# A Strassen-type transformer kernel: another order of the seven products, split token sums, block-diagonal gates, other store queues

## The chip, the cores and the metric

The kernel runs on one core of a Trainium2 chip. The metric is the device time of one execution in microseconds (us); the median of three runs counts. The engines are TensorE (PE, matrix products; PEld is its weight load), VectorE (DVE), ScalarE (ACT), GpSimd (POOL) and SyncE (SP), which issues most transfers; ACT and POOL issue some too. PSUM is the memory that TensorE writes, in 8 banks of 128 partitions x 512 fp32.

## The reference

There are two blocks of a network over one sequence of 1024 tokens of width 1024.

```python
h = rms_norm(x, norm1_g);  z = h @ w_in            # 1024 -> 3584
lru_x, lru_gate, sc_b, sc_c, sc_x = split(z)
lru_x = causal_dwconv(lru_x, lru_conv_w) + lru_conv_b
r = sigmoid(lru_x . wa + ba);  i = sigmoid(lru_x . wx + bx)   # 16 heads, 64 x 64 blocks
h_t = a_t * h_{t-1} + sqrt(1 - a_t^2) * (i * lru_x)_t         # a from r and lambda
y_lru = h * gelu(lru_gate);  y_sc = sc_b * causal_dwconv(sc_c * sc_x, sc_conv_w)
x = x + concat(y_lru, y_sc) @ w_out
u = causal_dwconv(rms_norm(x, norm2_g) @ w_up, ffn_conv_w);  gate, up = split(u)   # 1024 -> 6144
x = rms_norm(x + (gelu(gate) * up) @ w_down, final_g)
# second block: h = x @ w_in_2 gives q and kv of low rank, a pooled branch and two gates;
# attention of 4 heads with rope; layer_norm(alpha * x + concat(y_a, y_b) @ w_out_2)
```

## The kernel before

**Precision.** Each fp32 operand is held as a rounded part (hi, a CAST on ACT) and a rest (lo, a subtraction on DVE), and a product is three matmuls: hi·hi, hi·lo, lo·hi. `products` (L107) issues them at L110.

**Pairs.** The three stages of wide projections (the mix of block one, 14 pairs `wl*`, `ws*`, `wb*`; the ffn's `w_up`, 24 pairs `wf0` to `wf23`; block two's `w_in`, 9 pairs) work on pairs of 128 output columns by Strassen's scheme in Winograd's form: seven products of half width, each 12 matmuls of 128x512 into one PSUM bank. Products 1 and 2 share a bank (x), 6, 7 and 4 another (y), 5 and 3 a third (z). Later products of a bank add to what stands there, so what stands there must be read out (`evac`) before the next product of the bank starts. The tokens' operands (`Hop`) stay for the whole stage: product 1 reads B11, 2 reads B21 (both of tokens 0 to 511 alone), 5 reads T1, 6 T2, 7 T3, 4 T4 and 3 B22, sums in which tokens 512 to 1023 take part. The weights' operands are made for each pair: `load` fetches quarters, and their sums are formed in the DMA, by adding transfers that POOL issues (`sum`, L257 and L258, and L273). Product 5's operand is the tile `s`; once its lo part is done, an adding transfer turns `s` into 6's operand, and after 6's lo part another one turns it into 3's.

**Order of work.** Everything is emitted step by step, and each engine runs its own instructions in that order. `Pairs.step` emits the loads and sums of later pairs, the read-out of the product before, the hi and lo parts of the operand that is AHEAD products later, the product, and `tick()`, which emits the tasks that `later(n, ...)` put n steps ahead: convolutions, gates, scans, stores. ORDER is the order of the products in a pair, `prep_seq` that of the operands; the first two pairs of a stage run interleaved.

**Transitions.** `transition` leads into each stage: per tile of 128 tokens `norm.a` and `norm.b` (norm) and `norm.T` (transpose on PE, then the operands' parts). `T` of tiles 0 to 3 makes B11 and B21, `T` of tiles 4 to 7 the five others, nine DVE operations each (L443 to L462).

**Gates and late stages.** An lru pair's two gates multiply 64-row heads; the operands are stacked, hi over lo, so that eight matmuls do (`gates`), and eight sigmoids of 64 partitions read them (L666, L667). After the second stage `pooled_rows` fetches four tiles `yb` and four `wob`, splits each (`split`, L103 and L104) and multiplies them; `low_norm` (L1090) scales the fetched `lq`.

## Time and profile before

| | |
|---|---|
| median of 3 runs | 1858.32 us (1853.94 to 1858.72) |
| profiled execution | 1859.06 us, its span 1857.3 us |
| mean granted TensorE clock | 0.950 |
| PE / PEld / DVE / ACT / POOL busy | 1653.0 / 1351.0 / 1212.0 / 855.0 / 360.2 us |

Start and end of the span leave 1.8 us of the profiled time outside. Busy shares are means over stages with different limits, so they say little alone; the stages by time are: transition one to 77 us, the mix to about 404, its output rows to 524, transition two to 577, the ffn's pairs to 1060, its output rows to 1340, transition three to 1360, block two's pairs to 1538, the pooled rows to 1610, then q, k, v, attention and the last product. A share of granted clock of 1.00 is 2.4 GHz, 0.50 is 1.2 GHz.

### The profile page before, as it was taken

How to read it: one execution, taken by the hardware profiler on the slowest of the kernel's cores; microseconds unless marked ns; L12 is line 12 of the kernel's file. 1: busy time of each engine (PE TensorE's matmuls, PEld its weight loads, DVE VectorE, ACT ScalarE, POOL GpSimd, SP SyncE). 2: the span in 40 equal slices, each digit the busy share in tenths (PEclk: the TensorE clock that was granted, in tenths of full speed). 3: DMA queues.
4: the chain of work that ended last, by engine and by line, in shares of the span. 5: the costliest groups of instructions: out<-in, count | busy, mean ns of one | idle time of the engine just before them, and what ended most of it. 6: DMA issues, size and time to landing. Idle time of an engine off the chain costs nothing.

```text
span 1857.3 us, 20276 instructions
## 1 busy us (share of the span) xinstructions
PE 1653.0 (89%) x7315; PEld 1351.0 (73%) x7315; DVE 1212.0 (65%) x1729; ACT 855.0 (46%) x1290; POOL 360.2 (19%) x373
## 2 busy tenths in 40 slices
...
GB/s 208 87 101 85 114 128 107 72 182 226 125 108 89 164 125 135 143 148 144 125 134 144 166 334 123 102 54 10 124 127 129 184 72 283 215 108 266 92 99 118
DMA packets 272830, 255.36 MB, mean 137 GB/s; under 512 B 18422, under 2 KB 238420, under 8 KB 272724
## 3 DMA queue, kind: packets, MB, share of 16 engines
...
q14 instruction: 47, 0.39, 0.1%
...
## 4 chain that ended last, share of the span: by engine, by line
PE 45%; issue 22%; DMA 11%; DVE 11%; ACT 7%; POOL 3%; SPq 1%; POOLq 0%; DVEq 0%; ACTq 0%
PE o L110 22%; PE wu L110 4%; PE wob L110 2%; PE wl L110 2%; PE wq L110 2%; PE wga L110 2%; PE s L110 2%; PE ws L110 1%; PE qn L110 1%; PE wb L110 1%; PE wkv L110 1%; DVE B L443 1%; DVE T L443 1%; PE qr L110 1%; DVE ffc L758 1%
## 5 line engine op out<-in xcount | busy, mean ns | idle before, releaser
L110 PE MATMUL o<-yw 128*128 128x512 f32 x1632 | 375.3, 390 | 0.0
L110 PEld LDWEIGHTS o<-yw 128*128 128x128 f32 x1632 | 305.6, 188 | 63.6 <-DVE yw L524 0.8
L564 DVE TENSOR_TENSOR x<-x,o 128x512 f32<-128x512 f32 x160 | 108.6, 684 | 132.5 <-PE o L110 132.3
L523 ACT CAST yw<-yraw 128x1024 fp32r<-128x1024 f32 x34 | 35.7, 1051 | 174.4 <-PE o L110 152.4
L407 ACT ACTIVATE xn<-x 128x1024 f32<-128x1024 f32 x24 | 25.5, 1064 | 61.1 <-DVE x L564 54.3
L761 ACT ACTIVATE ffc<-ffc 128x1024 f32<-128x1024 f32 x24 | 25.4, 1059 | 58.5 <-DVE ffc L758 58.5
L524 DVE TENSOR_TENSOR yw<-yraw,yw 128x1024 fp32r<-128x1024 f32 x34 | 43.3, 1274 | 12.8 <-ACT yw L523 12.7
L524 DVE TENSOR_TENSOR yw<-wraw,yw 128x1024 fp32r<-128x1024 f32 x34 | 41.4, 1218 | 1.3 <-ACT yw L523 1.3
L436 PE MATMUL T<-cst,xn 128*128 128x128 f32 x128 | 20.7, 319 | 24.0 <-DVE xn L423 24.0
L523 ACT CAST yw<-wraw 128x1024 fp32r<-128x1024 f32 x34 | 35.8, 1053 | 11.2 <-DMA wraw<-in_w_out_dram 8.6
L110 PE MATMUL wob<-wobl,ybh 128*128 128x512 f32 x64 | 26.3, 410 | 15.3 <-DVE wobl L104 15.3
L1460 POOL TENSOR_TENSOR rt<-rt,lng 128x1024 f32<-128x1024 f32 x6 | 14.4, 2398 | 125.3 <-ACT rt L1459 125.3
L436 PEld LDWEIGHTS T<-cst,xn 128*128 128x128 f32 x128 | 18.0, 167 | 26.8 <-DVE xn L423 18.6
L668 POOL TENSOR_TENSOR i<-i,xc 128x1024 f32<-128x1024 f32 x8 | 19.6, 2448 | 77.7 <-ACT i L667 73.5
L110 PE MATMUL wob<-wobh,ybh 128*128 128x512 f32 x64 | 26.0, 413 | 9.3 <-ACT wobh L103 9.3
L257 POOL DMA_DIRECT2D wu3s<-in_w_in_dram x1 | 1.3, 1282 | 167.7 <-DMA wu3s<-in_w_in_dram 167.7
L110 PE MATMUL o<-PT,Vh 128*128 128x256 f32 x160 | 30.2, 287 | 4.0 <-DVE PT L1367 3.3
L1346 ACT ACTIVATE sc<-sc,st 128x256 f32<-128x256 f32 (+3 forms) x32 | 26.3, 823 | 15.2 <-DVE st L1345 15.1
L442 ACT CAST B<-T 128x512 fp32r<-128x512 f32 x36 | 20.8, 590 | 26.3 <-PE T L436 14.3
L417 POOL TENSOR_SCALAR ss<-ss 128x1 f32<-128x1 f32 x24 | 8.1, 339 | 117.7 <-ACT ss L408 116.9
L764 DVE TENSOR_TENSOR ffc<-ffc,ffc 128x1024 f32<-128x1024 f32 x24 | 29.3, 1222 | 1.9 <-ACT ffc L761 1.9
L110 PEld LDWEIGHTS o<-PT,Vh 128*128 128x128 f32 x160 | 25.3, 191 | 5.8 <-DVE PT L1367 4.2
...
## 6 DMA issues: line engine op xcount, KB each, us to landing
...
```

Source lines behind the costliest of these rows:

```text
L110: PE.matmul(ps, lhsT=l, rhs=r, start=(first and j == 0), stop=(last and j == n - 1), skip_group_check=not first)
L407: A.activation(xn, X[t], AF.Square, accum_out=ss[:, 0:1])
L436: PE.transpose(ps[:, k * P:(k + 1) * P], src[:, c * P:(c + 1) * P], ident)
L442: A.copy(Hop[m][:, 0, :, sl], src)
L443: V.tensor_tensor(Hop[m][:, 1, :, sl], src, f(Hop[m][:, 0, :, sl]), SUB)
L523: A.copy(s[:, j], src)
L524: V.tensor_tensor(s[:, j + 1], src, f(s[:, j]), SUB)
L564: V.tensor_tensor(X[t][:, ns], X[t][:, ns], ps, ADD)
L668: G.tensor_tensor(i, i, st.pop("xc"), MUL)
L761: A.activation(st["g"], st["g"], AF.Gelu_apprx_tanh)
L764: V.tensor_tensor(st["u"], st["u"], st["g"], MUL)
L1346: A.activation(s, s, AF.Exp, scale=QK_SCALE, bias=st[:, 1:2], accum_out=st[:, 2:3])
```

## The change

- Within a pair the products run 1, 6, 2, 7, 5, 4, 3 and no longer 6, 1, 5, 7, 2, 3, 4; operands are made 5 products ahead and not 6, in the order 5, 1, 2, 6, 7, 4, 3; loads and sums are emitted at other steps. Bank x is read out on ACT alone and the others on DVE alone, so product 6's read-out moves from ACT to DVE, product 1's loses its DVE addition, and the copy of product 5 and its later subtraction (L311, L317) fall away for all pairs but the first two of a stage. Between two products of one bank there now stands one other product, before there were two.
- In the first two pairs of a stage product 2 has a bank of its own (`apart`), and the order is 1, 2, 5, 3, 6, 7, 4, the two pairs in turn.
- `T` of tiles 4 to 7 makes only the parts of products 5 and 3; the new `T2` makes those of 6, 7 and 4, after two more steps of the products.
- The gates' weights are block-diagonal 128x128 tiles, with zeros put in by POOL; the gates take 12 matmuls, 4 sigmoids of 128 partitions and one split of `xc`, and their tasks come two steps earlier. The second and third pair of the mix change places.
- Stores of block two's pairs go out over POOL's or ACT's queue, not SP's.
- `pooled_rows` splits into four tiles of the pool H, not into 16 of the pool U.

```diff
-    ORDER = (6, 1, 5, 7, 2, 3, 4)
+    ORDER = (1, 6, 2, 7, 5, 4, 3)
...
-            if m in FIRST:
+            new = m in FIRST or m == 2 and self.apart
+            if new:
                 self.ps[g] = PB(self.nm)
+            self.bank[m] = self.ps[g]
             w, h = self.op.pop(m), Hop[m]
             terms = []
             for k in range(4):
                 terms += [(w[:, 0, k], h[:, 0, k]), (w[:, 0, k], h[:, 1, k]), (w[:, 1, k], h[:, 0, k])]
-            products(self.ps[g], terms, m in FIRST, True)
+            products(self.ps[g], terms, new, True)
...
             if m == 1:
                 A.copy(zb[:, n0], ps)
-                if 6 in self.seen:
-                    V.tensor_tensor(za[:, n1], za[:, n1], ps, ADD)
+            elif m == 2 and self.apart:
+                V.tensor_tensor(za[:, n0], ps, zb[:, n0], ADD)
             elif m == 2:
                 A.copy(za[:, n0], ps)
             elif m == 6:
-                if 1 in self.seen:
-                    V.tensor_tensor(za[:, n1], zb[:, n0], ps, SUB)
-                else:
-                    A.activation(za[:, n1], ps, AF.Copy, scale=-1.0)
+                V.tensor_tensor(za[:, n1], (za[:, n1] if 3 in self.seen else zb[:, n0]), ps, SUB)
...
+            elif 6 in self.seen:
+                V.tensor_tensor(za[:, n1], za[:, n1], ps, ADD)
             else:
-                V.tensor_tensor(za[:, n1], za[:, n1], ps, ADD)
+                V.tensor_tensor(za[:, n1], ps, zb[:, n0], ADD)
...
-        AHEAD = 6
+        AHEAD = 5
...
+            for p in pairs[:2]:
+                p.apart = True
+            self.seq = [(p, m) for m in (1, 2, 5, 3, 6, 7, 4) for p in pairs[:2]]
             self.seq += [(p, m) for p in pairs[2:] for m in ORDER]
-            early = (5, 1, 7, 2, 6, 4, 3)
-            self.prep_seq = [(p, m) for m in (1, 5, 2, 7, 6, 4, 3) for p in pairs[:2]]
-            self.prep_seq += [(p, m) for p in pairs[2:] for m in early]
+            self.prep_seq = [(p, m) for m in (1, 5, 2, 6, 3, 7, 4) for p in pairs[:2]]
+            self.prep_seq += [(p, m) for p in pairs[2:] for m in (5, 1, 2, 6, 7, 4, 3)]
...
-            self.load((g + 12) // 7 + 1)
-            self.sums((g + 9) // 7 + 1)
+            self.load(g // 7 + 3)
+            if g >= 3:
+                self.sums((g - 3) // 7 + 3)
...
-                Hop[6] = HB("T2")
-                Hop[5], Hop[7], Hop[4], Hop[3] = HT2("T1"), HT2("T3"), HT2("T4"), HT2("B22")
-            r = self.raw.pop(j)
+                Hop[5], Hop[3] = HT2("T1"), HT2("B22")
+            r = self.raw[j]
             q = U("hsum", F32, (P, 2, 4, P))
             V.tensor_tensor(q[:, 0], r[:, 0], v[0], SUB)
+            parts(5, q[:, 0])
+            parts(3, v[1])
             V.tensor_tensor(q[:, 1], v[1], q[:, 0], ADD)
-            parts(3, v[1])
-            for h in range(2):
-                V.tensor_tensor(r[:, h], r[:, h], q[:, 1], SUB)
-            parts(5, q[:, 0])
+            self.st[t] = q, parts
+
+        def T2(self, t):
+            q, parts = self.st.pop(t)
+            if t == 4:
+                Hop[6], Hop[7], Hop[4] = HB("T2"), HT2("T3"), HT2("T4")
+            r = self.raw.pop(t % 4)
             parts(6, q[:, 1])
+            V.tensor_tensor(r[:, 0], r[:, 0], q[:, 1], SUB)
             parts(7, r[:, 0])
+            V.tensor_tensor(r[:, 1], r[:, 1], q[:, 1], SUB)
             parts(4, r[:, 1])
...
         norm.T(7)
+        pairs.step()
+        pairs.step()
+        for t in range(4, NT):
+            norm.T2(t)
...
+            t = gwt[j] = U("gates", F32, (P, 8, P))
+            G.memset(t, 0.0)
             w = I[nm][0].rearrange("(c two) i j -> two i c j", two=2)
-            for rows_, half, col in zip((LOW, HIGH), (0, 1), cols):
-                SY.dma_start(t[rows_, :, col], w[half])
-
-    def stacked(src, rows_, hi, lo=None):
-
-        other = HIGH if rows_ == LOW else LOW
-        lo_t = hi if lo is None else lo
-        A.copy(hi[rows_], src[rows_])
-        V.tensor_tensor(lo_t[other], src[rows_], f(hi[rows_]), SUB)
-        if lo is not None:
-            A.copy(hi[other], src[rows_])
-            V.tensor_tensor(lo[rows_], src[rows_], f(hi[rows_]), SUB)
+            for half, r in enumerate((LOW, HIGH)):
+                SY.dma_start(t[r, :, r], w[half])
...
+            gw = U("gw", F32R, (P, 2, 2, P))
+            for j in range(2):
+                A.copy(gw[:, 0, j], gwt[j][:, c])
+                V.tensor_tensor(gw[:, 1, j], gwt[j][:, c], f(gw[:, 0, j]), SUB)
...
+        def cut():
+            st["xs"] = split(st["xc"], "xs")
 
         def gates():
             st["ps"] = [[PB("ga"), PB("ga")] for _ in range(2)]
+            (xh, xl), gw = st.pop("xs"), st.pop("gw")
             for j in range(2):
-                x = st.pop(f"xs{j}")
                 for n in range(2):
                     ns = slice(n * 512, (n + 1) * 512)
-                    products(st["ps"][j][n], [(st["gw"][:, 2 * j + part, :], x[:, ns]) for part in range(2)])
+                    products(st["ps"][j][n], [(gw[:, 0, j], xh[:, ns]), (gw[:, 0, j], xl[:, ns]), (gw[:, 1, j], xh[:, ns])])
...
+            for j, dst in enumerate((r, i)):
                 for n in range(2):
                     ns = slice(n * 512, (n + 1) * 512)
-                    ps = st["ps"][j][n]
-                    A.activation(r[own, ns], ps[own], AF.Sigmoid, bias=vcol(40 + c)[own])
-                    A.activation(i[own, ns], ps[other], AF.Sigmoid, bias=vcol(48 + c)[other])
+                    A.activation(dst[:, ns], st["ps"][j][n], AF.Sigmoid, bias=vcol(40 + 8 * j + c))
...
+            later(2, lambda: tap(zx, 1))
+            later(3, lambda: (tap(zx, 2), gelu(zg)))
             later(4, lambda: tap(zx, 3))
-            later(5, lambda: cut(0))
-            later(6, lambda: cut(1))
-            later(9, gates)
-            later(10, lru_1)
-            later(12, lru_2)
-            later(13, lru_3)
-            later(15, lru_4)
+            later(5, cut)
+            later(7, gates)
+            later(8, lru_1)
+            later(10, lru_2)
+            later(11, lru_3)
+            later(12, lru_4)
+            later(13, lru_5)
...
-    order = "L0 L1 S0 L2 S1 L3 B0 L4 S2 L5 L6 S3 L7 B2"
+    order = "L0 S0 L1 S1 L2 L3 B0 L4 S2 L5 L6 S3 L7 B2"
...
-            store(YB_d[g], t)
+            store(YB_d[g], t, G)
...
-            store(GA_d[h + j], z)
+            A.dma_start(GA_d[h + j], z)
...
-            y[e] = split(y[e], "yb")
-            w[e] = split(w[e], "wob")
+            s = HT("yw", F32R, (P, 4, 1024))
+            for j, src in ((0, y[e]), (2, w[e])):
+                A.copy(s[:, j], src)
+                V.tensor_tensor(s[:, j + 1], src, f(s[:, j]), SUB)
+            y[e], w[e] = (s[:, 0], s[:, 1]), (s[:, 2], s[:, 3])
```

On ACT, where pair 16's products of the ffn run (`COPY` reads out a bank; L266 before and L260 after are the hi parts; `wf17s` is the tile that the transfers add to). Before, with product 1's read-out of pair 16 at the top:

```order
L293 COPY wf16z_6291<-wf_856_6296 128x512
L266 CAST wf17op_6324<-wf17a_6171 128x512
L761 ACTIVATE ffc_6310<-ffc_6310 128x1024
L311 COPY wf16m_863_6340<-wf_862_6326 128x512
L266 CAST wf17op_6343<-wf17s_6173 128x512
L266 CAST wf17op_6361<-wf17a_6171 128x512
L266 CAST wf17op_6380<-wf17s_6173 128x512
L266 CAST wf17op_6398<-wf17b_6176 128x512
L297 COPY wf16z_6290<-wf_856_6296 128x512
L266 CAST wf17op_6415<-wf17s_6173 128x512
L754 ACTIVATE ffc_6430<-wf16z_6291,fvec 128x1024
```

and of the change, with product 1's read-out of pair 16 at the top:

```order
L289 COPY wf16z_6175<-wf_832_6159 128x512
L260 CAST wf16op_6178<-wf16s_5872 128x512
L750 ACTIVATE ffc_6194<-wf15z_6035,fvec 128x1024
L260 CAST wf17op_6199<-wf17s_6011 128x512
L260 CAST wf17op_6219<-wf17a_6009 128x512
L260 CAST wf17op_6236<-wf17a_6009 128x512
L293 COPY wf16z_6174<-wf_832_6159 128x512
L757 ACTIVATE ffc_6194<-ffc_6194 128x1024
L260 CAST wf17op_6254<-wf17s_6011 128x512
L260 CAST wf17op_6272<-wf17s_6011 128x512
L260 CAST wf17op_6296<-wf17b_6014 128x512
L750 ACTIVATE ffc_6311<-wf16z_6175,fvec 128x1024
```

The hi parts of pair 17 stand in the order of `prep_seq`: before 5, 1, 7, 2, 6, 4, 3, in the change 5, 1, 2, 6, 7, 4. Before, that of product 3 (the last from `wf17s`) stands three rows behind that of product 6; now it stands past the end of these rows, behind pair 17's own read-out of product 1, and that of product 6 stands behind pair 16's read-out of product 2.

On PE, at transition two (`T<-cst,xn` are transposes of the last tiles, `wf` is the bank; B_515 and B_506 are B11, B_516 and B_507 are B21, T_545 and T_563 are T2, T_546 and T_536 are T1). Before:

```order
L110 MATMUL wf_556_3902<-B_515_3663,wf0op_3527 128x512 x12
L436 MATMUL T_3915<-cst,xn_3778 128x128 x4
L436 MATMUL T_3920<-cst,xn_3778 128x128 x4
L110 MATMUL wf_563_3946<-B_515_3663,wf1op_3530 128x512 x12
L436 MATMUL T_3959<-cst,xn_3823 128x128 x4
L436 MATMUL T_3964<-cst,xn_3823 128x128 x4
L110 MATMUL wf_556_3902<-B_516_3664,wf0op_3545 128x512 x12
L110 MATMUL wf_563_3946<-B_516_3664,wf1op_3897 128x512 x12
L110 MATMUL wf_575_4031<-T_545_3845,wf0op_3995 128x512 x12
L110 MATMUL wf_577_4050<-T_545_3845,wf1op_4012 128x512 x12
L110 MATMUL wf_579_4067<-T_546_3846,wf0op_3535 128x512 x12
L110 MATMUL wf_582_4085<-T_546_3846,wf1op_3541 128x512 x12
```

and of the change:

```order
L110 MATMUL wf_546_3807<-B_506_3583,wf0op_3447 128x512 x12
L431 MATMUL T_3820<-cst,xn_3698 128x128 x4
L431 MATMUL T_3825<-cst,xn_3698 128x128 x4
L110 MATMUL wf_553_3843<-B_506_3583,wf1op_3450 128x512 x12
L431 MATMUL T_3856<-cst,xn_3743 128x128 x4
L431 MATMUL T_3861<-cst,xn_3743 128x128 x4
L110 MATMUL wf_560_3880<-B_507_3584,wf0op_3465 128x512 x12
L110 MATMUL wf_562_3900<-B_507_3584,wf1op_3805 128x512 x12
L110 MATMUL wf_567_3928<-T_536_3765,wf0op_3455 128x512
L110 MATMUL wf_570_3954<-T_536_3765,wf1op_3461 128x512
L110 MATMUL wf_567_3928<-T_536_3765,wf0op_3455 128x512 x11
L110 MATMUL wf_570_3954<-T_536_3765,wf1op_3461 128x512 x11
```

Product 2 writes other banks (`wf_560`, `wf_562`) than product 1 (`wf_546`, `wf_553`), and the products that follow it are those of T1, before they were those of T2.

On DVE, at the pooled rows (L104 and L1134 are lo parts, L1090 and L1086 the scaling of `lq`). Before:

```order
L313 TENSOR_TENSOR wga2z_10582<-wga_1414_10564,wga2z_10582 128x512
L1090 SCALAR_TENSOR_TENSOR lq_10750<-lq_10750,vec,linv_10748 128x1024
L1090 SCALAR_TENSOR_TENSOR lq_10752<-lq_10752,vec,linv_10748 128x1024
L1090 SCALAR_TENSOR_TENSOR lq_10754<-lq_10754,vec,linv_10748 128x1024
L1090 SCALAR_TENSOR_TENSOR lq_10756<-lq_10756,vec,linv_10748 128x1024
L104 TENSOR_TENSOR ybl_10767<-yb_10732,ybh_10766 128x1024
L104 TENSOR_TENSOR wobl_10771<-wob_10734,wobh_10770 128x1024
L104 TENSOR_TENSOR ybl_10799<-yb_10736,ybh_10798 128x1024
L104 TENSOR_TENSOR wobl_10803<-wob_10738,wobh_10802 128x1024
```

and of the change:

```order
L307 TENSOR_TENSOR wga2z_10418<-wga2z_10418,wga_1388_10472 128x512
L1134 TENSOR_TENSOR yw_10603<-yb_10569,yw_10603 128x1024
L1134 TENSOR_TENSOR yw_10603<-wob_10571,yw_10603 128x1024
L1134 TENSOR_TENSOR yw_10632<-yb_10573,yw_10632 128x1024
L1134 TENSOR_TENSOR yw_10632<-wob_10575,yw_10632 128x1024
L1134 TENSOR_TENSOR yw_10661<-yb_10577,yw_10661 128x1024
L1134 TENSOR_TENSOR yw_10661<-wob_10579,yw_10661 128x1024
L1134 TENSOR_TENSOR yw_10690<-yb_10581,yw_10690 128x1024
L1134 TENSOR_TENSOR yw_10690<-wob_10583,yw_10690 128x1024
L1086 SCALAR_TENSOR_TENSOR lq_10587<-lq_10587,vec,linv_10585 128x1024
L1086 SCALAR_TENSOR_TENSOR lq_10589<-lq_10589,vec,linv_10585 128x1024
```

The four scalings of `lq` stood ahead of the first lo part; now they stand behind the eighth.

## Rows read from the trace of the kernel before

**Rows 1.** Busy time of each engine by stretch. Columns: stretch in us, its length, busy us (instructions) of PE, PEld, DVE, ACT and POOL, granted clock, share of the DMA engines' time, GB/s.
```profile
0.00:77.44 77.44, 39.31 (x163) 32.55 (x164) 45.24 (x77) 40.69 (x79) 23.70 (x54) 0.69 0.67 154
77.44:404.00 326.56, 281.20 (x1151) 223.43 (x1150) 230.65 (x276) 219.94 (x314) 93.63 (x60) 0.94 0.53 101
...
524.00:577.06 53.06, 41.53 (x195) 34.08 (x194) 49.01 (x80) 34.97 (x68) 11.86 (x44) 0.87 0.37 115
577.06:1060.00 482.94, 452.93 (x1956) 367.60 (x1955) 326.37 (x438) 216.14 (x329) 112.79 (x87) 0.99 0.69 137
...
1360.00:1540.00 180.00, 178.17 (x786) 147.20 (x784) 111.77 (x152) 83.34 (x129) 34.70 (x27) 1.00 0.65 135
1540.00:1610.00 70.00, 47.18 (x192) 38.15 (x192) 31.62 (x27) 14.66 (x14) 0.00 (x0) 0.80 0.70 259
```

**Rows 2.** Waits of PE in the ffn's stretch (577 to 1060), by what ended them: us in total, times, longest. The first of twenty rows of this kind, one for each of pairs 3 to 23 but one.
```profile
PE wf L110 <- DVE wf8z L295: 2.9, 1, 2.9
```

**Rows 3.** PE in order of time around pair 17 of the ffn: start, us, engine, line, operation, output and inputs, count, and in brackets the idle time before and what ended it.
```profile
918.44 2.88 PE L110 MATMUL wf<-T,wf17op 128*128 128x512 f32 x12
...
921.16 2.88 PE L110 MATMUL wf<-B,wf17op 128*128 128x512 f32 x12
...
930.97 5.78 PE L110 MATMUL wf<-B,wf17op 128*128 128x512 f32 x24 [1.48 <-DVE wf17z L295]
```

**Rows 4.** DVE, POOL and ACT in the same stretch, columns as above, put in order of time.
```profile
913.63 0.68 DVE L271 TENSOR_TENSOR wf17op<-wf17s,wf17op 128x512 fp32r<-128x512 f32 x1
...
914.61 1.28 POOL L273 DMA_DIRECT2D wf17s<-in_w_up_dram  x1 [3.40 <-DVE wf17op L271]
...
920.83 0.62 ACT L266 CAST wf17op<-wf17s 128x512 fp32r<-128x512 f32 x1 [7.04 <-DMA wf17s<-in_w_up_dram]
...
921.48 0.69 DVE L271 TENSOR_TENSOR wf17op<-wf17s,wf17op 128x512 fp32r<-128x512 f32 x1 [5.96 <-ACT wf17op L266]
...
930.23 0.68 DVE L295 TENSOR_TENSOR wf17z<-wf17z,wf 128x512 f32<-128x512 f32 x1
```

**Rows 5.** Transfers: from issue to landing of the adding transfers of L273 at 900 to 935 us (three of them), and the median for pair 21's four issues.
```profile
DMA to landing us min/median/max: 4.3/4.6/6.2
...
wf21s<-in_w_up_dram POOLq DMA_DIRECT2D x4, 256.0 KB, 6.5
```

**Rows 6.** The transitions: waits of PE in transition one (columns as in rows 2), PE in order of time in transition two (columns as in rows 3), and the waits in transition three.
```profile
PE wl L110 <- ACT wl0z L293: 6.7, 1, 6.7
PE wl L110 <- ACT wl1z L293: 6.3, 1, 6.3
...
551.19 2.98 PE L110 MATMUL wf<-B,wf1op 128*128 128x512 f32 x12
...
561.30 5.43 PE L110 MATMUL wf<-B,wf0op 128*128 128x512 f32 x12 [6.25 <-ACT wf0z L293]
...
572.00 5.21 PE L110 MATMUL wf<-B,wf1op 128*128 128x512 f32 x12 [5.28 <-ACT wf1z L293]
...
593.40 2.88 PE L110 MATMUL wf<-B,wf0op 128*128 128x512 f32 x12
...
PE wu L110 <- ACT wu3z L293: 6.4, 1, 6.4
PE wkv L110 <- ACT wkvz L293: 5.8, 1, 5.8
```

**Rows 7.** A stretch of transition two by engine (columns as in rows 1), and ACT's read-out of product 1 of pair 0 (columns as in rows 3). The stretch begins with DVE's first sum for tile 4 (L458).
```profile
549.66:575.73 26.07, 14.54 (x53) 11.17 (x53) 26.05 (x44) 15.77 (x30) 3.65 (x8) 0.76 0.38 85
...
560.67 0.58 ACT L293 COPY wf0z<-wf 128x512 f32<-128x512 f32 x1
```

**Rows 8.** Waits of PE in the mix (77 to 404 us), columns as in rows 2: the longest, and the longest of two other kinds.
```profile
PE ws L110 <- ACT ws1op L266: 9.4, 1, 9.4
PE ws L110 <- DVE ws2z L295: 4.2, 1, 4.2
...
PE ws L110 <- ACT ws2z L302: 3.1, 1, 3.1
```

**Rows 9.** ACT in the mix: groups of equal shape, with busy us, mean ns, and idle time before them with what ended it; the last row is the cast L103 at the pooled rows, with min, median and max ns.
```profile
L667 ACT ACTIVATE i<-ga,vec 64x512 f32<-64x512 f32 x28 | 19.1, 684 | 1.7 <-DVE sco L718 1.3
...
L615 ACT CAST xs<-xc 64x1024 fp32r<-64x1024 f32 x14 | 14.6, 1046 | 17.6 <-DVE xc L641 13.2 <-PE ws L110 4.3
...
L103 ACT CAST ybh<-yb x4: 1044/1044/1044, 1545.1 to 1553.2; 128x1024 fp32r<-128x1024 f32 x4
```

**Rows 10.** ACT, PE and DVE at the pooled rows, columns as in rows 3.
```profile
1545.13 1.04 ACT L103 CAST ybh<-yb 128x1024 fp32r<-128x1024 f32 x1 [5.14 <-DMA yb<-YB]
...
1554.51 1.04 ACT L103 CAST wobh<-wob 128x1024 fp32r<-128x1024 f32 x1 [0.29 <-DMA wob<-in_w_out_dram]
...
1547.51 1.65 PE L110 MATMUL wob<-wobh,ybh 128*128 128x512 f32 x3 [9.34 <-ACT wobh L103]
...
1557.08 3.78 DVE L1090 SCALAR_TENSOR_TENSOR lq<-lq,vec,linv 128x1024 f32<-128x1024 f32 x3 [18.18 <-DMA lq<-LQ]
...
1564.46 0.80 PE L110 MATMUL wob<-wobl,ybh 128*128 128x512 f32 x1 [15.30 <-DVE wobl L104]
...
1570.12 0.39 PE L110 MATMUL wob<-wobl,ybh 128*128 128x512 f32 x1
...
1609.81 0.39 PE L110 MATMUL wob<-wobh,ybl 128*128 128x512 f32 x1
```

More of the change, by code (lines that the diff above doesn't have):

```diff
@@ L238, in __init__ @@
             self.ap, self.cols, self.nm, self.done = ap, (c0, c1), nm, done
-            self.op, self.ps, self.z, self.seen = {}, {}, None, []
+            self.op, self.ps, self.z, self.seen, self.apart, self.bank = {}, {}, None, [], False, {}
         def load(self):
@@ L282, in product @@
                 terms += [(w[:, 0, k], h[:, 0, k]), (w[:, 0, k], h[:, 1, k]), (w[:, 1, k], h[:, 0, k])]
-            products(self.ps[g], terms, m in FIRST, True)
+            products(self.ps[g], terms, new, True)
         def evac(self, m):
-            ps = self.ps[GROUP[m]]
+            ps = self.bank.pop(m)
             n0, n1 = slice(0, 512), slice(512, 1024)
@@ L322 @@
     class Pairs:
-        AHEAD = 6
+        AHEAD = 5
         def __init__(self, pairs):
             self.pairs = pairs
-            self.seq = [(p, m) for m in (1, 2) for p in pairs[:2]]
-            self.seq += [(p, m) for m in (6, 5, 7, 3, 4) for p in pairs[:2]]
+            for p in pairs[:2]:
+                p.apart = True
+            self.seq = [(p, m) for m in (1, 2, 5, 3, 6, 7, 4) for p in pairs[:2]]
             self.seq += [(p, m) for p in pairs[2:] for m in ORDER]
-            early = (5, 1, 7, 2, 6, 4, 3)
-            self.prep_seq = [(p, m) for m in (1, 5, 2, 7, 6, 4, 3) for p in pairs[:2]]
-            self.prep_seq += [(p, m) for p in pairs[2:] for m in early]
+            self.prep_seq = [(p, m) for m in (1, 5, 2, 6, 3, 7, 4) for p in pairs[:2]]
+            self.prep_seq += [(p, m) for p in pairs[2:] for m in (5, 1, 2, 6, 7, 4, 3)]
             self.n_load, self.n_sum, self.n_prep, self.n_prod, self.n_evac = 0, 0, 0, 0, 0
@@ L485, in transition @@
         norm.T(7)
+        pairs.step()
+        pairs.step()
+        for t in range(4, NT):
+            norm.T2(t)
+            pairs.step()
     class Rows:
@@ L604, in gate_weights_load, with store @@
     def gate_weights_load():
-        t = gwt["raw"] = U("gates", F32, (P, 8, P))
-        for nm, cols in (("lru_wa", (LOW, HIGH)), ("lru_wx", (HIGH, LOW))):
+        for j, nm in enumerate(("lru_wa", "lru_wx")):
+            t = gwt[j] = U("gates", F32, (P, 8, P))
+            G.memset(t, 0.0)
             w = I[nm][0].rearrange("(c two) i j -> two i c j", two=2)
-            for rows_, half, col in zip((LOW, HIGH), (0, 1), cols):
-                SY.dma_start(t[rows_, :, col], w[half])
-    def stacked(src, rows_, hi, lo=None):
-        other = HIGH if rows_ == LOW else LOW
-        lo_t = hi if lo is None else lo
-        A.copy(hi[rows_], src[rows_])
-        V.tensor_tensor(lo_t[other], src[rows_], f(hi[rows_]), SUB)
-        if lo is not None:
-            A.copy(hi[other], src[rows_])
-            V.tensor_tensor(lo[rows_], src[rows_], f(hi[rows_]), SUB)
+            for half, r in enumerate((LOW, HIGH)):
+                SY.dma_start(t[r, :, r], w[half])
     stored = set()
-    def store(dst, t):
+    def store(dst, t, E=SY):
         def go():
-            SY.dma_start(dst, t)
+            E.dma_start(dst, t)
             stored.add(id(dst))
```

32 lines of the change are left out of this document (8 added, 24 removed).

## Prediction

> **What bounds the kernel now.** I read the busy times by stretch first. They tell the reader to look at five places and to leave the rest. In the second block's pairs PE works 178.2 of 180 us at full clock [rows 1]: nothing is to be gained there, only lost. In the ffn's pairs it stands idle 482.9 - 452.9 = 30.0 us, in the mix 326.6 - 281.2 = 45.4 us, at the pooled rows 70.0 - 47.2 = 22.8 us with a granted clock of 0.80, and in transition two 53.1 - 41.5 = 11.5 us at 0.87 [rows 1]. So PE bounds the kernel, and what a change is worth is the idle time, and the low clock behind it, that it takes from PE.
>
> Then the waits. In the ffn nearly every pair has one wait of the same kind: PE stands before product 2 until DVE has added product 1 from the bank (L295) [rows 2]; in pair 17 it is 1.48 us [rows 3]. DVE in order of time shows why it is late. The lo part of product 6 is done at 914.3, POOL issues the adding transfer at 914.61, and ACT's next hi part from that tile waits until 920.83, 7.04 us; DVE then waits 5.96 us for it, and all that stands behind it is late, L295 too, at 930.23 [rows 4]. The landing is what ends last: 4.3 to 6.2 us from issue, with 6.5 as a later pair's median [rows 5].
>
> In transition two PE waits for ACT's read-out of product 1, which stands in ACT's queue behind parts that DVE's sums must feed [rows 6, 7]. DVE is busy 26.05 of 26.07 us, 44 operations, 0.59 us each [rows 7]: it is the bound there. The products after the waits take 5.43 and 5.21 us against 2.98 [rows 6]: the lower level of the clock, 1.2 GHz. Transition one has waits of 6.7 and 6.3 us, three of 6.4 and 5.8 [rows 6].
>
> At the pooled rows PE begins at 1547.51 and is stopped at once until 1564.46, for `wobl` [rows 10]. All casts are done by 1555.6, but DVE stood 18.18 us in L1090 for the fetched `lq`, ahead of the lo parts [rows 10].
>
> **The change, part by part.** The sum is made against the profiled execution, 1859.06 us; it lies 0.7 above the median of 1858.32.
>
> *Order in the ffn.* Twelve matmuls take 921.16 - 918.44 = 2.72 us [rows 3]. Count from the start of a pair's product 1; product 3, seventh, would start at 6 x 2.72 = 16.32, and needs bank z, so the read-out of product 5, which ends at 13.6. On DVE that read-out stands behind the next pair's lo parts of 6 and 7, and 6's waits for an adding transfer, issued after 5's lo part. The read-out of product 6 (free at 5.44) and 5's lo part take 0.68 each; with some queueing the latter is done at about 7.65. POOL's issue comes 0.3 later [rows 4], the landing 4.3 to 6.2 after it [rows 5]: 12.3 to 14.2. Then hi 0.62, two lo parts and the read-out, 0.65 each: done at 14.8 to 16.7. PE waits 0 to 0.4 us. The other transfer, for 3's operand, is followed by product 1's read-out, and 3 comes last, so it has some three products more than before. A pair loses 0.2 us instead of 30.0 / 20 = 1.5: 24 pairs, 30.0 - 24 x 0.2 = **-25 us** (-30 if no landing is late). What covers this is bank slack: one product, 2.72 us, from the end of a product to the next of its bank, where two stood before. ACT loses two copies a pair, and DVE the same number as it gains, so neither becomes fuller.
>
> The Trainium skill (DMA: Bandwidth & Descriptors, Anatomy of one DMA) gives such a transfer as about 2.0 us plus its bytes at 436 GB/s; for 256 KB that is an estimate of 2.6 us. This case's rows show 4.3 to 6.2 instead [rows 5], so the measurement decides; by the page's figure the landing would never end last and the ffn would give the whole 30.
>
> *Transitions.* Product 2 now has its own bank and reads B21, ready before the late tiles. After product 1 of the second pair (551.19 + 2.72) and the last transposes, to 555, both products 2 run to 560.5. DVE has 17 operations and a norm (1.3) from 549.66 on: 17 x 0.6 + 1.3 gives 561.2; both products 5 run to 567.5. Product 3 needs two adding transfers one behind the other; the second follows 6's lo part at 562.5, lands at 567.1 to 569.3, and hi and lo make it 568.5 to 570.5; both products 3 end at 574 to 576. `T2`'s parts for 6 need 12 more DVE operations, 7.2 us behind that, 576.7; both products 6 end by 582. The same ten products ended at 593.4 [rows 6]: -11. For transition one and three, with waits of 13.0 and 12.2 us, I take -10 and -7: **-28 us** (-36 if all idle and low-clock time goes; -12 if the two landings keep the parts back at each).
>
> *Mix.* The gates add 4 matmuls to each of 8 pairs: 32 x 0.2267 = +7.3 us. ACT's sigmoids cost the same for 64 as for 128 partitions would: the cast of 64x1024 takes 1046 ns, that of 128x1024 1044 [rows 9]. So a gate pair saves ACT 4 x 0.68 + 1.05 + 2 x 0.3 us, and the two copies, 1.2: 5.6 of some 26. The longest wait, 9.4 us, is for a hi part behind two lru pairs' sigmoids at a time [rows 8]; with an S pair between L0 and L1 they fall apart. The read-outs that PE waits for next, L295 and L302 [rows 8], are gone in this form, but others with half the slack take their place. Of 45.4 us idle I leave 25: **-13 us** (-25 to +10; the gates' own 7.3 and shorter slack behind ACT's bursts are the upper end).
>
> *Pooled rows.* DVE's lo parts follow the casts; PE runs from about 1549 at the loads' pace. From 1564.46 on it took 45.6 us to 1610.1, with 14 matmuls to 1570.12 at the lower clock [rows 10]. The same from 1549 to 1550 on gives 1596: **-13 us** (-7 to -15: the stores of YB now stand in POOL's queue, and later loads may keep their times).
>
> *Second block's pairs.* There is nothing to win; the bank slack and the stores that stand ahead of adding transfers on POOL can cost 0 to 1 us a pair: **+3 us** (0 to +10).
>
> Sum: -25 - 28 - 13 - 13 + 3 = -76, so **1783 us**.
>
> **The rivals.**
> - *The landing still ends last in the ffn* (the accumulates follow one another as closely, DMA engines are 0.69 busy there [rows 1]): the wait goes over to bank z, 1.5 us a pair as now. Ffn 0: 1808 us. For it: 6.5 us medians [rows 5]; against: the chain above has 2.7 us more room.
> - *Slower: the lost slack is paid.* If the late landing stays as it is and hits a read-out with one product of slack where two stood, a pair's wait is 1.5 + 2.72 = 4.2 us: +2.72 x 22 = +60 in place of -25. 1783 + 25 + 60 = 1868 us. By the walk the wait is the landing less 5.8, so it takes landings of about 10 us in every pair; none of those read is over 6.5 [rows 5].
> - *The mix gets worse*: ACT's bursts (4 sigmoids and two table loads in one go) exceed 2.7 us of slack in each of 14 pairs by 1 to 2 us more than before. Mix +15: 1811 us.
> - *The transitions do not change much*: DVE's total there is the same, 26 us [rows 7], and product 3 waits for two landings. -8 in place of -28: 1803 us.
>
> **How the numbers follow.** Chances: forecast 0.55, ffn rival 0.14, slower 0.09, mix 0.12, transitions 0.10. The time is the forecast's, 1783; alone its terms reach from 1765 to 1800. The range takes in the rivals of 1803, 1808 and 1811 with a part of two of them together: 1760 to 1828. Two of a kind that add up to over 1864 are rare beside the slower rival itself. Faster by over 0.3% (5.6 us, about what a measurement of this kernel can tell from no change): 0.86; within it 0.04; slower 0.10.
>
> **What would show it.** In the profile of the changed kernel: idle PE in the ffn's stretch near 5 us instead of 30, with DVE's read-out of product 5 as what ends the little that is left; no wait of PE for a read-out of product 1 in the transitions, and the first products 2 directly behind the transposes; `wob` products from about 1549 without a stop; 25 us of idle PE in the mix, the 9.4 us wait gone; second block's PE still over 98% busy. The prediction is wrong if PE waits for L300 (product 5) or for a read-out of product 1 in every pair, for more than 1 us.

## The result, and the profile of the changed kernel

The changed kernel takes 1777.9 us (median of 4 runs, 1775.12 to 1785.59) against 1858.35 us: a ratio of 0.9579 (95% interval 0.9545 to 0.9612). The profiled execution takes 1776.74 us, its span is 1774.6 us, the mean granted clock 0.973 (0.950 before), PE is busy 1635.7 us.

The busy times by stretch, columns as in [rows 1]. Here the stretches end with events, so that they answer to the same work in both kernels: to the end of pair 0 of the mix; to the mix's last product; from the ffn's first product to pair 1's last; pairs 2 to 23; block two's pairs from the third on; the pooled rows. First the changed kernel:

```profile
0.00:91.86 91.86, 58.16 (x259) 47.90 (x259) 54.65 (x95) 46.32 (x91) 30.23 (x59) 0.83 0.72 160
91.86:375.00 283.14, 258.58 (x1105) 206.86 (x1106) 208.26 (x246) 180.37 (x238) 91.08 (x57) 0.99 0.59 119
513.74:562.90 49.16, 42.05 (x190) 33.42 (x189) 40.61 (x67) 24.29 (x44) 14.53 (x19) 1.00 0.67 132
562.90:989.42 426.52, 420.81 (x1848) 345.79 (x1847) 319.25 (x423) 189.57 (x273) 104.25 (x81) 1.00 0.74 149
1303.51:1465.48 161.97, 154.59 (x667) 125.27 (x665) 99.82 (x135) 69.04 (x102) 35.63 (x34) 0.99 0.56 117
1465.48:1521.47 55.99, 47.03 (x193) 37.88 (x192) 33.10 (x28) 15.75 (x15) 0.00 (x0) 0.91 0.87 308
```

and the kernel before, for the first, second and fourth of them:

```profile
0.00:99.49 99.49, 61.36 (x260) 50.82 (x261) 60.46 (x115) 50.33 (x99) 28.86 (x58) 0.76 0.67 145
99.49:411.70 312.21, 266.85 (x1085) 211.05 (x1084) 221.20 (x245) 217.62 (x303) 88.47 (x56) 0.94 0.53 107
...
604.44:1063.20 458.76, 428.75 (x1849) 347.57 (x1849) 316.39 (x422) 209.13 (x316) 106.45 (x82) 0.99 0.69 140
```

The stages by such events, in us; what lies between and behind them, the ffn's output rows, attention and the last product, takes 428 us in both kernels (1857.3 - 1428.9 and 1774.6 - 1346.4) and is left out. The rows from the third on are of kernels that the next section describes:

| | to end of pair 0 | to ffn's first product | transition two | ffn 2 to 23 | transition three | block two's rest | pooled rows | to q | q, k, v |
|---|---|---|---|---|---|---|---|---|---|
| before | 99.5 | 448.1 | 56.9 | 458.8 | 56.6 | 151.5 | 72.0 | 7.0 | 78.5 |
| changed | 91.9 | 421.9 | 49.2 | 426.5 | 47.2 | 162.0 | 56.0 | 11.7 | 80.0 |
| e_ffn_old | 91.7 | 423.0 | 50.0 | 470.4 | 48.1 | 164.3 | 55.7 | 10.8 | 80.5 |
| e_ahead6 | 92.1 | 428.8 | 48.0 | 489.4 | 49.6 | 165.8 | 54.8 | 11.7 | 78.8 |
| e_ahead4 | 90.7 | 427.6 | 45.2 | 428.0 | 45.2 | 162.5 | 56.0 | 10.4 | 77.8 |
| e_prep_old | 92.2 | 430.2 | 49.2 | 428.0 | 46.8 | 156.8 | 56.2 | 12.9 | 78.6 |
| e_no_apart | 97.3 | 421.7 | 50.7 | 425.3 | 45.6 | 164.1 | 56.4 | 12.5 | 78.8 |
| e_one_stage | 97.5 | 423.7 | 56.6 | 431.5 | 54.6 | 163.9 | 56.1 | 11.6 | 79.6 |
| e_mix_old | 92.2 | 434.1 | 48.6 | 425.3 | 47.2 | 163.5 | 55.7 | 12.5 | 78.6 |
| e_gates_old | 88.5 | 430.6 | 51.0 | 425.0 | 47.1 | 162.8 | 55.7 | 11.0 | 82.1 |
| e_mix_order | 92.3 | 426.2 | 50.2 | 423.1 | 46.7 | 162.1 | 55.5 | 12.7 | 78.9 |
| e_second_old | 94.1 | 424.0 | 49.4 | 424.0 | 52.0 | 151.7 | 54.6 | 11.7 | 78.6 |
| e_rr_pool | 94.0 | 426.1 | 53.4 | 423.1 | 47.3 | 162.8 | 55.7 | -0.2 | 84.6 |
| e_best | 90.4 | 426.1 | 45.0 | 428.0 | 45.8 | 155.2 | 54.7 | -0.2 | 83.5 |

A negative figure means that the q products begin before the pooled rows' last. The column "q, k, v" ends with the first score product. Where nothing of a stage was edited, a profile differs from the changed kernel's by up to 5 us, so differences of that size show nothing by themselves.

The ffn's waits in the changed kernel, as in [rows 2], the first and the last of seven:

```profile
PE wf L110 <- DVE wf14z L300: 1.2, 1, 1.2
...
PE wf L110 <- DVE wf6z L297: 0.5, 1, 0.5
```

Pair 17 of [rows 3, 4] is made ready while pair 16 runs. In order of time: PE's product 1 of pair 16, POOL's adding transfer for 17's product 6, ACT's hi part behind it, DVE's read-out of 16's product 5 (L300), and product 3:

```profile
834.54 2.88 PE L110 MATMUL wf<-B,wf16op 128*128 128x512 f32 x12
...
842.45 1.28 POOL L267 DMA_DIRECT2D wf17s<-in_w_up_dram  x1 [8.38 <-DVE wf17op L265]
...
849.31 1.14 ACT L260 CAST wf17op<-wf17s 128x512 fp32r<-128x512 f32 x2 [4.22 <-DMA wf17s<-in_w_up_dram]
...
851.18 0.68 DVE L300 TENSOR_TENSOR wf16z<-wf16z,wf 128x512 f32<-128x512 f32 x1
...
852.01 2.97 PE L110 MATMUL wf<-B,wf16op 128*128 128x512 f32 x12 [0.98 <-DVE wf16z L300]
```

From product 1's start these are 7.9, 14.8, 16.6 and 17.5 us: the walk of the prediction with a landing of 6.9 us, and a wait of 0.98 us. That is one of the late ones: PE waits in seven of the 22 pairs, 5.7 us in all.

### The profile page after: what moved, and what is told of

It reads as the page before. It is cut to its first block, busy times and chain, and to the rows that moved or that the text cites. A ratio compares the mean times of both kernels' runs of the same rounds, so it can differ in the third digit from the quotient of the medians.

```text
span 1774.6 us, 20249 instructions
## 1 busy us (share of the span) xinstructions
PE 1635.7 (92%) x7347; PEld 1339.8 (75%) x7347; DVE 1191.5 (67%) x1711; ACT 778.3 (44%) x1147; POOL 371.6 (21%) x387
## 3 DMA queue, kind: packets, MB, share of 16 engines
q10 hardware_dynamic: 720, 2.18, 0.4%
## 5 line engine op out<-in xcount | busy, mean ns | idle before, releaser
L110 PE MATMUL wob<-yw 128*128 128x512 f32 x192 | 47.0, 408 | 9.0 <-DVE yw L1134 8.9
L110 PEld LDWEIGHTS wob<-yw 128*128 128x128 f32 x192 | 37.9, 199 | 18.1 <-ACT yw L1133 9.3
```

Of the source, the lines that this page charges most:

```text
L110: PE.matmul(ps, lhsT=l, rhs=r, start=(first and j == 0), stop=(last and j == n - 1), skip_group_check=not first)
```

## The experiments

Each kernel is the changed one with one edit; e_best joins three. Medians are of 4 runs, 10 for e_ahead6 and 5 for e_best; the ratio, with its 95% interval, is to the kernel before.

### e_ffn_old

```diff
-    ffn = Pairs([ff_pair(fi) for fi in range(NF)])
+    ffn = Pairs([ff_pair(fi) for fi in range(NF)], old=True)   # ORDER, prep_seq, AHEAD, load, sums, evac of before
```

> The changed kernel, but the ffn's pairs from the third on keep the order of before: products 6, 1, 5, 7, 2, 3, 4, operands 5, 1, 7, 2, 6, 4, 3, six ahead, loads and sums at the old steps. If the order within a pair carries the ffn's gain (458.8 to 426.5 us for pairs 2 to 23 by the two profiles), the time is 1778 + 32 = 1810 us (1803 to 1815), with the waits of PE for L295 back, 1.5 us in most pairs. If the gain came from other edits (transfers, queues, the transition that hands over), it stays within 5 us of 1778.

Measured: 1825.81 us, 0.9823 (0.9801 to 0.9845): +47.9 us. The ffn's pairs took 470.4 us, and every other stage stayed within 2.5 us. What `old=True` takes back in one edit (the order of products and operands, 6 ahead, the steps of loads and sums, the read-outs) carries all of the ffn's gain; the next runs take parts of it apart. The stretch is even 11.6 us longer than in the kernel before; the waits for the read-out of product 1 are as there, and waits for L307, product 5's copy, come on top (5.1 us in pair 7). Why the same order costs more here than there is open.

### e_prep_old

```diff
-            self.prep_seq += [(p, m) for p in pairs[2:] for m in (5, 1, 2, 6, 7, 4, 3)]
+            self.prep_seq += [(p, m) for p in pairs[2:] for m in (5, 1, 7, 2, 6, 4, 3)]
```

> The changed kernel with its product order and banks, but the operands of all pairs from the third on are made in the old order 5, 1, 7, 2, 6, 4, 3, so that the hi part of 3's operand again stands close behind the lo part of 6's, with an adding transfer of 4 to 6.5 us between. Theory (the place of the transfer carries the gain, and a late landing now meets one product of bank slack): ACT waits about 7 us in each pair again, and PE 1.5 to 4.2 us: 22 ffn pairs x 1.2 to 3.9 = +26 to +86 us there alone, 1805 us or more. Rival (the product order and the banks carry the gain, not the operand order): within 5 us of 1778.

Measured: 1782.17 us, 0.9597 (0.9574 to 0.962). The theory as I put it here fell: the ffn is 428.0 us, unchanged. In its profile 3's hi part does not stand close behind 6's: with five ahead it comes after its own pair's read-out of product 1, in either order of operands, and ACT waits 66 us for the pairs' transfers (67 in the changed kernel). So it is not the order of the operands that moves it. In the other stages the edit does something by this profile: the mix is 8.3 us longer and block two's pairs are 5.2 us shorter.

To read these runs, one thing said ahead of the prediction has to be put more exactly: an engine's queue is not quite in the order of emission. By the source, the read-out of product 5 is emitted ahead of the hi and lo parts of 6's operand; in the rows of pair 16 above it runs behind them. How the program comes to that order is not shown here. The waits follow the order of the queues.

### e_ahead6 and e_ahead4

```diff
-        AHEAD = 5
+        AHEAD = 6    # e_ahead4: 4
```

> The changed kernel with operands made 6 products ahead again, all else as it is. Theory (what spares the ffn is that 3's hi part comes one product later than before, behind the landing of its adding transfer; with 6 ahead ACT meets it while the transfer is under way): ACT's waits for transfers in the ffn rise from 69 to some 150 us again, the read-outs are late, and the ffn gains 10 to 40 us: 1788 to 1818 us. Rival (the product order alone carries the ffn's gain, by putting 3 last): within 5 us of 1778.

> The changed kernel with operands made 4 products ahead. If the waits are only those of hi parts for transfers (ACT 69 us in the ffn at 5 ahead, some 150 at 6), each product less helps: ffn -3 to -6 us, 1772 to 1775. If 5 is where two limits meet, hi and lo parts now come too late for their own products behind ACT's and DVE's other work: PE waits for lo parts (L265), +5 to +40 us.

Measured: 1849.87 us with 6 (0.9951, 0.9931 to 0.9971), 1774.28 us with 4 (0.9547, 0.9531 to 0.9563). One number gives back 72 of the 80 us, more than the 10 to 40 expected, and 62.9 of them in the ffn's pairs, 2.9 us a pair. In e_ahead6's pair 17, in order of time: product 1, the adding transfer for 18's product 6, ACT's hi parts behind it, DVE's read-out of product 7 (L297) and PE's product 4:

```profile
906.95 2.88 PE L110 MATMUL wf<-B,wf17op 128*128 128x512 f32 x12
...
912.05 1.28 POOL L267 DMA_DIRECT2D wf18s<-in_w_up_dram  x1 [10.47 <-DVE wf18op L265]
...
918.37 1.14 ACT L260 CAST wf18op<-wf18s 128x512 fp32r<-128x512 f32 x2 [5.27 <-DMA wf18s<-in_w_up_dram]
...
921.16 0.68 DVE L297 TENSOR_TENSOR wf17z<-wf,wf17z 128x512 f32<-128x512 f32 x1
...
921.90 1.43 PE L110 MATMUL wf<-T,wf17op 128*128 128x512 f32 x5 [1.19 <-DVE wf17z L297]
```

The transfer starts 2.8 us earlier in the pair than with 5 ahead (5.1 against 7.9) and lands in 6.3 us, but the lo parts that wait for it now stand ahead of product 7's read-out on DVE, not of product 5's. That one is late by 1.19 us. And the second transfer's hi part, for product 3, now stands ahead of product 5's read-out:

```profile
903.34 0.68 DVE L300 TENSOR_TENSOR wf16z<-wf16z,wf 128x512 f32<-128x512 f32 x1
...
904.08 3.04 PE L110 MATMUL wf<-B,wf16op 128*128 128x512 f32 x12 [1.50 <-DVE wf16z L300]
```

So most of the 22 pairs have two waits (17 for L297, 19.0 us in all, and 18 for L300, 33.5 us), where most had one before the change and seven have one in the changed kernel; ACT waits 170 us for the pairs' transfers (67 with 5 ahead, 147 before the change). With 6 ahead the new order is slower than the old one with 6 (489.4 against 470.4 us in e_ffn_old and 458.8 before), so the ffn's gain needs the 5. The old order with 5 ahead was not run; what share of the gain is the order's own is open.

With 4 ahead the time is the expected one but for another reason: the ffn gains nothing more (428.0), the transitions gain 7 us in all, and the mix loses 5.7.

### e_no_apart and e_one_stage

```diff
 # e_no_apart
-                p.apart = True
+                p.apart = False
 # e_one_stage
             self.st[t] = q, parts
+            self.T2(t)
...
-        pairs.step()
-        pairs.step()
-        for t in range(4, NT):
-            norm.T2(t)
-            pairs.step()
```

> The changed kernel, but product 2 of each stage's first two pairs adds into product 1's bank again; the sums stay in two stages. Theory (the own bank takes away PE's wait for ACT's read-out of product 1): two waits of up to 6 us in each of three transitions come back in part, +10 to +20 us, 1788 to 1798. Rival (the two stages of the sums carry the transitions' gain, 23 us by the profiles, because ACT's read-out is then early enough): within 5 us of 1778.

> The changed kernel, but all five sums of a late tile are made at once again, right behind its transposes, with no product between; product 2 keeps its own bank. Theory (DVE's work in a transition is the same, the two stages only let products 5 and 3 start before the rest is done): PE waits for DVE's 12 operations of about 0.6 us more before product 5, some 5 to 7 us in each of three transitions less what products 3 and 6 then save, +6 to +15 us in all, 1784 to 1793. Rival (the own bank alone carries the transitions): within 5 us of 1778.

Measured: 1780.97 us (0.9589, 0.9554 to 0.9625) without the own bank, 1802.1 us (0.9692, 0.9669 to 0.9714) with one stage. By its profile the own bank is worth 5.4 us in transition one, of which 1.9 us is a wait of PE for the read-out of product 1, and nothing that shows in the others; its median, 3.1 us above the changed kernel's, can't be told from nothing. The two stages are worth 5.6, 7.4 and 7.4 us in the three transitions. With one stage these take 97.5, 56.6 and 54.6 us, about what they took before (99.5, 56.9 and 56.6), although product 2 has its own bank. In e_one_stage's transition two, product 2 of pair 0, DVE's lo part for pair 1's product 2, and that product:

```profile
528.65 3.00 PE L110 MATMUL wf<-B,wf0op 128*128 128x512 f32 x12
...
537.83 0.68 DVE L265 TENSOR_TENSOR wf1op<-wf1a,wf1op 128x512 fp32r<-128x512 f32 x1
...
538.56 4.63 PE L110 MATMUL wf<-B,wf1op 128*128 128x512 f32 x10 [5.21 <-DVE wf1op L265]
```

PE waits 5.21 us, not for a bank but for a lo part that stands on DVE behind the sums; DVE works without a pause from 523 us on. In two stages fewer sums stand ahead of it.

### e_mix_old, e_gates_old and e_mix_order

```diff
 # e_mix_old
-    mix = Pairs([kinds[w[0]](int(w[1:])) for w in order.split()])
+    mix = Pairs([kinds[w[0]](int(w[1:])) for w in order.split()], old=True)
 # e_mix_order
-    order = "L0 S0 L1 S1 L2 L3 B0 L4 S2 L5 L6 S3 L7 B2"
+    order = "L0 L1 S0 L2 S1 L3 B0 L4 S2 L5 L6 S3 L7 B2"
 # e_gates_old: gate_weights_load, stacked, conv_0, cut, gates, lru_1 to lru_4, their steps and vec_load as before
```

> The changed kernel, but the mix's pairs from the third on keep the order of before and 6 ahead; gates, pair order and transition as changed. The stretch from the end of pair 0 to the ffn's first product went from 448.1 to 421.9 us by the two profiles, where the prediction had about 13 for gates, pair order and products together. Theory (the order and 5 ahead carry most of it, as in the ffn): +15 to +25 us, 1793 to 1803. Rival (gates and pair order carry it, some 5 us each by their runs, and the order the rest): +5 to +12, 1783 to 1790.

> The changed kernel with the gates of before: stacked operands, 8 matmuls and 8 sigmoids of 64 partitions a pair, their tasks two steps later. Theory (ACT's and DVE's savings of 5 us a pair are worth more than the 32 matmuls more, 7.3 us): +5 to +20 us in the mix, 1783 to 1798. Rival (ACT is not the bound of the mix after the new order, so that only the matmuls count): -7 us, 1771.

> The changed kernel with the pairs of the mix in the order of before, L0 L1 S0 L2 S1. Theory (two lru chains one behind the other fill ACT's queue, which made the longest wait of before, 9.4 us): +5 to +12 us, 1783 to 1790. Rival (with fewer sigmoids the two chains fit): within 4 us of 1778.

Measured: 1790.51 us (0.9634, 0.9618 to 0.965), 1779.67 us (0.9566, 0.9537 to 0.9595), 1782.39 us (0.9593, 0.9574 to 0.9612). The products' order, with 5 ahead, is worth 12.6 us by the medians and 12.2 by the stage, less than the theory's 15. The pair order's 4.5 and 4.3 us are no more than stages differ by without an edit. The gates' 1.8 us by the medians can't be told from nothing; their stages show 8.7 us in the mix and -3.4 at the start, a net 5.3.

### e_second_old, e_rr_pool and e_best

```diff
 # e_second_old: block two's Pairs(..., old=True)
 # e_rr_pool
-            SY.dma_start(R3_d[t], r)
+            G.dma_start(R3_d[t], r)
 # e_best: both, and in step()
-            self.prep(g + self.AHEAD)
+            self.prep(g + (4 if g < 10 else self.AHEAD))
```

> The changed kernel, but block two's pairs from the third on keep the order of before and 6 ahead; stores stay on POOL's and ACT's queues. By the two profiles these pairs went from 151.5 to 162.0 us. Theory (one product of bank slack in place of two costs them this): -8 to -11 us, 1767 to 1770. Rival (the stores on POOL stand ahead of adding transfers and cost it): within 4 us of 1778.

Measured: 1771.43 us, 0.9536 (0.9516 to 0.9556), 6.5 us less than the changed kernel; block two's pairs from the third on are back at 151.7 us, as before, with the stores where the change put them. So the order, with the operands' order and 5 ahead, costs the 10.5 us there, and the stores on POOL do not. In the changed kernel PE had six waits in this stretch, of which the first two:

```profile
PE wu L110 <- ACT wkrh L103: 3.5, 1, 3.5
PE wq L110 <- DVE wqz L300: 1.0, 1, 1.0
```

The first is put down to a cast that the waiting product does not read. Around it, ACT's hi parts, DVE's read-out of product 5 and product 3 of that pair:

```profile
1344.18 1.14 ACT L260 CAST wqop<-wqs 128x512 fp32r<-128x512 f32 x2 [6.30 <-DMA wqs<-in_w_in_dram]
...
1345.44 0.68 DVE L300 TENSOR_TENSOR wu2z<-wu2z,wu 128x512 f32<-128x512 f32 x1
...
1346.27 4.17 PE L110 MATMUL wu<-B,wu2op 128*128 128x512 f32 x12 [3.45 <-ACT wkrh L103]
```

The product begins 0.15 us after the read-out ends, as in pair 16 of the ffn. By these times it is the ffn's wait once more: a read-out of product 5 behind lo parts that wait for a transfer, here one of 5.9 us (issued at 1338.24).

The expected 8 to 11 us did not all arrive: in this run, with 6 ahead, transition three took 4.8 us more.

> The changed kernel with the eight stores of the pooled rows' sums on POOL's queue, which is idle there, not on SP's. Theory (the first q weights are fetched behind these stores on SP, and PE waits 11.7 and 5.1 us for them): the fetch comes early, -8 to -14 us, 1764 to 1770. Rival (the fetches behind wait for free tiles, not for the stores, or the wait goes over to the rotation of the keys): within 3 us of 1778.

Measured: 1775.79 us, 0.9548 (0.9532 to 0.9563): 2.1 us less, within what a measurement can tell, and the expected 8 us are not in the median. The profile shows the fetch itself early. SP in the changed kernel, the last store and the fetch of `wqr` behind it, PE's wait for it, and then SP and PE in e_rr_pool:

```profile
1526.13 0.34 SPq L1149 DMA_DIRECT2D RR<-rx  x1
...
1526.57 1.47 SPq L1168 DMA_DIRECT2D wqr<-in_w_uq_dram  x2
...
1533.21 0.80 PE L110 MATMUL qr<-lqh,wqrh 128*128 128x512 f32 x1 [11.75 <-ACT wqrh L103]
```

```profile
1514.37 1.23 SPq L1168 DMA_DIRECT2D wqr<-in_w_uq_dram  x2
...
1534.60 0.79 PE L110 MATMUL qr<-lqh,wqrl 128*128 128x512 f32 x1 [4.99 <-DVE wqrl L104]
```

From the start of the pooled rows to the first score product it took 140.1 instead of 147.7 us; part of the wait went over to `wqrl`, 4.99 us, behind DVE's other work. Its other stages, not edited, were longer in this profile (mix and transition two by 4 us each), and it is open whether that is chance.

> The changed kernel with what the runs so far favour put together: block two's pairs from the third on in the order of before and 6 ahead (-10.3 us in those pairs by its profile), the pooled rows' stores on POOL's queue (-7.6 us from the pooled rows to the first score product by its profile), and operands 4 ahead in the first ten steps of each stage (the three transitions were 7 us shorter in all at 4 ahead), 5 ahead after that. If these add up: 1778 - 10 - 8 - 7 = 1753 us. Rival (they hide behind one another, as the medians of the single runs, 1771.4, 1775.8 and 1774.3, already show less than their stages): the sum of the medians' gains, 6.5 + 2.1 + 3.6 = 12, 1766 us, or less.

Measured: 1760.85 us (1759.22 to 1761.73), 0.948 (0.9467 to 0.9493): 17 us below the changed kernel, the fastest of all here. It lies between the two expectations. Block two's pairs took 155.2 us here against 151.7 in e_second_old with the same order; one wait of PE for a read-out of product 1, 1.8 us, is half of that, and the rest is not explained.

## Why the prediction was right, point by point

The time is 1777.9 where 1783 was forecast, and all five places moved; the errors partly cancel. By the two profiles the ffn and the mix gave 23 us more than forecast, while transitions, block two's pairs, the stretch behind the pooled rows and the mix's output rows (+2.9) gave 20 less, with 3 more at the pooled rows: that the sum came within 6 us is in part luck.

- **ffn, -25 forecast, -32.2 measured.** The walk holds almost to the tenth in pair 16 (issue at 7.9, wait 0.98 where 0 to 0.4 stood, for a landing of 6.9 us), and the idle time left is 5.7 us where it had 5. The term was too small because it counted idle time alone: 30.0 us of idle stood for 458.8 - 22 x 19.04 = 39.9 us lost, and now 7.6 us are lost. Of the other 9.9 us 3.5 are the lower clock, which was granted behind the two longest waits and nowhere else in the stretch. Below, the two waits, and the clock from the end of each on and between them:

```profile
677.93 7.33 PE L110 MATMUL wf<-B,wf5op 128*128 128x512 f32 x24 [2.75 <-DVE wf5z L295]
...
742.87 7.35 PE L110 MATMUL wf<-B,wf8op 128*128 128x512 f32 x24 [2.86 <-DVE wf8z L295]
...
677.50:682.00 4.50, 4.07 (x12) 3.28 (x13) 4.50 (x14) 2.09 (x3) 0.72 (x1) 0.68 1.18 145
682.00:742.50 60.50, 55.84 (x241) 44.89 (x240) 44.14 (x69) 29.35 (x43) 14.16 (x12) 1.00 0.68 138
742.50:747.00 4.50, 4.13 (x12) 3.27 (x13) 4.50 (x8) 3.42 (x6) 1.43 (x2) 0.67 1.30 164
```

  These 24 matmuls took 7.33 and 7.35 us, where 24 in a row take 5.60 else. Another 3.4 are the ends of the products ahead of the 21 waits: twelve matmuls take 2.88 us to their end but 2.72 to the next product's start, and where PE waits that 0.16 us is paid and counted as busy. The last 3 us lie in the products right behind a wait, which take a little longer (24 matmuls 5.78 us in [rows 3]). The step left open what puts the transfer at its place. By e_prep_old it is not the operand order; by e_ahead6 it is the number of products ahead, in this product order.
- **Transitions, -28 forecast, -24.7 measured** (7.6, 7.7 and 9.4). The order of events in transition two came as walked: both products 2 with no wait over 0.43 us, 5 behind them, then a wait before 3 and before 6:

```profile
521.29 3.00 PE L110 MATMUL wf<-B,wf0op 128*128 128x512 f32 x12
...
528.03 2.65 PE L110 MATMUL wf<-T,wf0op 128*128 128x512 f32 x11
...
536.29 3.02 PE L110 MATMUL wf<-B,wf0op 128*128 128x512 f32 x12 [2.66 <-ACT wf0m L303]
...
543.73 2.83 PE L110 MATMUL wf<-T,wf0op 128*128 128x512 f32 x11 [1.70 <-DVE T L438]
```

  Moved by the 33.8 us that this kernel is ahead here, these are 555.1, 561.8, 570.1 and 577.5, where the walk had 555, 561 to 562, 568.5 to 570.5 and 576.7. The wait before product 3 ends with ACT's copy of product 5 (`wf0m`), for which the walk had no term. That copy stands on ACT behind the hi parts of both products 3, and these wait for their transfers, so the landing still decides, by way of ACT's queue:

```profile
533.39 0.62 ACT L260 CAST wf0op<-wf0s 128x512 fp32r<-128x512 f32 x1 [2.20 <-DMA wf0s<-in_w_up_dram]
...
535.14 0.62 ACT L260 CAST wf1op<-wf1s 128x512 fp32r<-128x512 f32 x1 [0.61 <-DMA wf1s<-in_w_up_dram]
535.66 0.58 ACT L303 COPY wf0m<-wf 128x512 f32<-128x512 f32 x1
```

  It is the same in transitions one and three, where PE waits 4.7 and 3.0 us for this copy. The ten products end at 549.1, moved 582.9, where the walk had 582; the ten that ended at 593.4 before were 1, 2, 6, 5 and 7 of both pairs and not the same ones. Of these 10 to 11 us, 7.7 are left at the end of the transition, as the four products behind have a wait of 2.18 us for a read-out (L297). And the part that carries the gain is the two stages, which the prediction used for the dates of products 5 and 6 without a price of their own; the own bank, its first step, is worth little by e_no_apart.
- **Mix, -13 forecast, -29 measured** for 312.2 to 283.1 us. The idle time fell from 45.4 to 24.6 us, and 25 was the figure left. This is beyond the step's bound of -25. What it left out is the low clock behind the waits: the granted clock rose from 0.94 to 0.99, and PE's busy time fell by 8.3 us although it does 28 gate matmuls more in this stretch, 6.3 us. The sigmoids' price held: 64 partitions took 684 ns [rows 9], 128 now take 686 to 692:

```profile
L661 ACT ACTIVATE i<-ga,vec 128x512 f32<-128x512 f32 x14 | 9.0, 692 | 0.0
```

- **Pooled rows, -13 forecast, -16.0 measured**, but 4.7 and 1.5 us are given back behind them: the q weights' fetch stands behind the last store on SP, and that store waits for the fetch of its own `rx`. The prediction named later loads that keep their times only as a bound. The mechanism is the forecast's by the profile, though no run takes this edit back alone: all lo parts run ahead of the scaling of `lq`, and PE, once it has begun, is not stopped again:

```profile
1474.40 47.06 PE L110 MATMUL wob<-yw 128*128 128x512 f32 x192 [8.91 <-DVE yw L1134]
...
1482.11 1.23 DVE L1134 TENSOR_TENSOR yw<-wob,yw 128x1024 fp32r<-128x1024 f32 x1 [0.15 <-ACT yw L1133]
1483.61 5.07 DVE L1086 SCALAR_TENSOR_TENSOR lq<-lq,vec,linv 128x1024 f32<-128x1024 f32 x4 [0.28 <-DMA lq<-LQ]
```

- **Block two's pairs, +3 forecast, +10.5 measured**: the upper bound. PE is busy 154.6 of 162.0 us, 95%, where over 98% was to be seen. One product of bank slack, which the prediction priced at 0 to 1 us a pair, did not cover the longest wait there, 3.45 us behind a landing of 5.9 us.
- **The slower rival** was no idle one. With 6 ahead its mechanism, a read-out late behind a transfer with one product of slack, makes the ffn 30.6 us longer than before, 1849.9 us in all. Its condition was put too narrowly: the landings need not be 10 us (6.3 in the rows above), it is enough that one more read-out stands behind them.

The Trainium skill (DMA: Bandwidth & Descriptors, Anatomy of one DMA) would have these transfers land in 2.6 us, an estimate by its formula; the changed kernel's in the ffn took 4.4 to 8.6 us, and the measurement decides:

```profile
DMA to landing us min/median/max: 4.4/5.1/8.6
```
